# RMS norms of a two-layer decoder step: partial sums on VectorE, a root without ScalarE, and one tile per step for the second half's first norm

## Chip, cores and metric

The kernel runs on one core of a Trainium2 chip. The metric is device time in microseconds (us) of one execution.

## What is computed

One inference step of a two-layer decoder on 1024 prompt tokens and 8 sequences of 8 sampled tokens. Layer 0 mixes tokens by stick-breaking attention, layer 1 by an RWKV-7 recurrence; each is followed by a squared-ReLU MLP. Every sub-layer starts with an RMS norm whose result is scaled and shifted by vectors computed from a conditioning input, and ends with a gated residual add:

```python
def rmsnorm(x, g):
    y = x * lax.rsqrt(jnp.mean(x * x, axis=-1, keepdims=True) + 1e-6)
    return y * g
...
for i in range(2):
    hp, gp = ada_norm(xp, c, norm_mix[i], ...)      # norm 0 (attention), norm 2 (RWKV)
    xp = xp + gp * mixer(hp)                        # w_o is the mixer's last matmul
    hp, gp = ada_norm(xp, c, norm_ffn[i], ...)      # norms 1 and 3
    u = relu(hp @ w_up[i])
    xp = xp + gp * ((u * u) @ w_down[i])
y = rmsnorm(xp, final_norm)                         # the final norm
```

## The kernel before

**Tiling.** Activations lie transposed: 8 tiles of 128 features by tokens. The 1088 tokens are cut into half A (576, all prompt) and half B (448 prompt and 64 sampled tokens). Each half has 5 norms, so there are 10. They are called 0A, 0B, 1A, 2A, 1B, 2B, 3A, 3B, FA and FB below (F: final), which is their order in time except that FA comes just behind 3B.

**A dense layer** (`dense`, L346 to L362) is done in three products, because each fp32 operand is split into a high and a low part: for each output tile `m` and each stretch of tokens, 8 steps of three matmuls into `dq` (L358 high by high, L359 weight by low part of the input, L360 low part of the weight). The weights are split as they come: ScalarE casts `wh` (L342), GpSimd and VectorE subtract `wl` (L344, L345). After each step `self.step` lets other work go on by its rate: attention, then the RWKV units (`rw_units`, whose VectorE rows here are L1046 to L1163, and their triangular inverses `rw_lanes`, L1205 to L1214), then the RWKV chains. The evacuation of `w_o` and `w_down` is `residual` (L363): VectorE adds gate times `dq` to the x tile (L373); for sampled tokens VectorE makes `rs` (L376) and GpSimd adds it (L379).

**A norm** (`rms`, L258) squares the 8 tiles of x on ScalarE (`sq`, L265) and sums over features on TensorE: 4 matmuls with a matrix of ones for each tile, 32 in all, into `ssq` (L267). A program's fp32 matmul shows as two records. ScalarE takes a square root (L271), and VectorE turns it into a reciprocal root with one Newton step (L272 to L277, tile `rv`). Four matmuls spread the result over the partitions (`rb`, L281), and four copies, alternately on ScalarE and VectorE, make the tile `R`. Then `norm_tiles` makes for each tile x times R (`hf`, L291 on VectorE; for sampled tokens L295 to L297 on GpSimd), adds the shift and splits into `hhi` (ScalarE, L323 and L132) and `hlo` (VectorE L324, GpSimd L304); `rw_norm` does the like for norm 2 (`h`). The next dense layer's first matmul needs the first `hhi`, its second matmul the first `hlo`.

**Order.** The kernel is written with a tile framework whose scheduler sets the order of the instructions on each engine; each engine then works through its own list in that order. While half A goes through its first dense layers, the norm of half B's input runs beside it (`second`, at rate 1/5 of a step): all of `rms` in one step of that generator, then one tile of the norm per step. x is streamed for it tile by tile (`Passing`, L102, DMAs issued by SyncE). FA runs beside the last MLP of half B.

## Time and profile before

| | |
|---|---|
| median of 3 runs | 3694.59 us (3686.51 to 3700.34) |
| the profiled execution | 3691.91 us, of which its span is 3690.2 us |
| mean granted TensorE clock | 0.967 |
| busy share: TensorE, VectorE, ScalarE, GpSimd | 94%, 63%, 43%, 33% |
| instructions in all | 72202 |
| start of the ten square roots (L271) in norm order 0A to FB | 16.9, 67.7, 734.1, 1370.4, 1791.8, 2272.8, 2638.4, 3295.7, 3320.8, 3677.1 us |

The profile is one execution. Engines: PE is TensorE's matmul, PEld its weight load, DVE is VectorE, ACT is ScalarE, POOL is GpSimd, SP is SyncE. L267 is line 267 of the kernel. In a row of a timeline stand start, duration, engine, line, operation, output and inputs, and in square brackets how long the engine was idle before it and what ended that. A row of the waits names who waited for whom, the total, the number of times and the longest. PEclk is the clock granted to TensorE as a share of full speed. Idle time costs something only where TensorE, the busiest engine, has to wait.

### The profile page before, as it was taken

How to read it: one execution, taken by the hardware profiler on the slowest of the kernel's cores; microseconds unless marked ns; L12 is line 12 of the kernel's file. 1: busy time of each engine (PE TensorE's matmuls, PEld its weight loads, DVE VectorE, ACT ScalarE, POOL GpSimd, SP SyncE). 2: the span in 40 equal slices, each digit the busy share in tenths (PEclk: the TensorE clock that was granted, in tenths of full speed). 3: DMA queues.
4: the chain of work that ended last, by engine and by line, in shares of the span. 5: the costliest groups of instructions: out<-in, count | busy, mean ns of one | idle time of the engine just before them, and what ended most of it. 6: DMA issues, size and time to landing. Idle time of an engine off the chain costs nothing. (4 is left out here: it accounts for less than half of the span.)

```text
span 3690.2 us, 72202 instructions
## 1 busy us (share of the span) xinstructions
PE 3482.2 (94%) x26360; PEld 2770.2 (75%) x26360; DVE 2306.5 (63%) x4718; ACT 1602.1 (43%) x3342; POOL 1223.3 (33%) x1692
## 2 busy tenths in 40 slices
PE   7999999999999999988799998998899999989998
PEld 5986667778888876766577776666788888867887
DVE  4357678885554446687845557657884666645444
ACT  4255566663333345634334445543433444432332
POOL 2344434342222223223433335323222222343332
PEclk8999999999999999988899998999899999989999
DMA  6466653319977785667254445657345444433332
GB/s 237 147 218 209 208 182 121 96 38 333 350 290 263 276 315 174 206 192 210 79 155 133 122 153 159 192 190 219 117 132 144 140 132 122 125 113 114 95 95 83
DMA packets 433014, 634.54 MB, mean 172 GB/s; under 512 B 144337, under 2 KB 244562, under 8 KB 432658
## 3 DMA queue, kind: packets, MB, share of 16 engines
q1 hardware_dynamic: 369394, 532.90, 44.8%
q10 hardware_dynamic: 63264, 97.02, 7.9%
q8 instruction: 209, 3.42, 0.4%
q14 instruction: 147, 1.20, 0.1%
HBM read 523.76 MB, written 106.01 MB: 171 GB/s over the span
## 5 line engine op out<-in xcount | busy, mean ns | idle before, releaser
L344 POOL TENSOR_TENSOR wl<-wst,wh 128x256 fp32r<-128x256 f32 (+1 forms) x512 | 652.7, 1276 | 1432.1 <-ACT wh L342 1214.9
L342 ACT CAST wh<-wst 128x512 fp32r<-128x512 f32 (+1 forms) x512 | 424.5, 834 | 709.9 <-PE dq L359 570.2
L358 PE MATMUL dq<-hhi,wh 128*128 128x288 f32 (+1 forms) x2112 | 711.5, 337 | 21.1 <-ACT hhi L132 19.1
L359 PE MATMUL dq<-hlo,wh 128*128 128x288 f32 (+1 forms) x2112 | 704.0, 334 | 3.7 <-DVE hlo L324 2.9
L360 PE MATMUL dq<-hhi,wl 128*128 128x288 f32 (+1 forms) x2112 | 703.2, 333 | 0.0
L345 DVE TENSOR_TENSOR wl<-wst,wh 128x256 fp32r<-128x256 f32 (+1 forms) x512 | 358.8, 703 | 258.7 <-ACT wh L342 230.4
L358 PE MATMUL dq<-uh,wh 128*128 128x288 f32 (+1 forms) x1536 | 508.9, 336 | 5.3 <-ACT uh L472 2.2
L359 PE MATMUL dq<-ul,wh 128*128 128x288 f32 (+1 forms) x1536 | 507.2, 331 | 0.0
L360 PE MATMUL dq<-uh,wl 128*128 128x288 f32 (+1 forms) x1536 | 505.4, 332 | 0.0
L358 PEld LDWEIGHTS dq<-hhi,wh 128*128 128x128 f32 x2112 | 400.9, 190 | 71.0 <-ACT hhi L132 19.7
L359 PEld LDWEIGHTS dq<-hlo,wh 128*128 128x128 f32 x2112 | 401.0, 190 | 43.3 <-issue 9.3
L360 PEld LDWEIGHTS dq<-hhi,wl 128*128 128x128 f32 x2112 | 400.5, 190 | 36.2 <-issue 6.9
L373 DVE SCALAR_TENSOR_TENSOR x<-dq,mod,x 128x288 f32<-128x288 f32 (+1 forms) x432 | 245.2, 569 | 258.6 <-PE dq L360 255.5
L358 PEld LDWEIGHTS dq<-uh,wh 128*128 128x128 f32 x1536 | 288.1, 188 | 53.6 <-issue 18.0
L548 DVE TENSOR_TENSOR_SCAN prod<-prod 128x256 f32<-128x256 f32 (+5 forms) x264 | 247.9, 941 | 118.0 <-ACT prod L539 76.8
L360 PEld LDWEIGHTS dq<-uh,wl 128*128 128x128 f32 x1536 | 288.4, 188 | 29.6 <-issue 7.1
L359 PEld LDWEIGHTS dq<-ul,wh 128*128 128x128 f32 x1536 | 288.8, 188 | 27.6 <-issue 5.7
L358 PE MATMUL dq<-xhi,wh 128*128 128x288 f32 (+1 forms) x576 | 203.1, 353 | 4.8 <-ACT dn L132 1.8
L359 PE MATMUL dq<-xlo,wh 128*128 128x288 f32 (+1 forms) x576 | 199.7, 347 | 5.8 <-POOL xlo L304 3.9
L360 PE MATMUL dq<-xhi,wl 128*128 128x288 f32 (+1 forms) x576 | 197.5, 343 | 0.0
L470 DVE TENSOR_TENSOR ut<-ut 128x288 f32<-128x288 f32 (+1 forms) x192 | 154.2, 803 | 53.0 <-ACT ut L469 50.1
L472 ACT CAST uh<-ut 128x288 fp32r<-128x288 f32 (+1 forms) x192 | 94.8, 495 | 181.6 <-DVE ut L470 181.2
(300 smaller groups left out, 6234.7 us busy)
## 6 DMA issues: line engine op xcount, KB each, us to landing
pagek<-cache_kT SPq DMA_DIRECT2D x128, 512.0 KB
pagev<-cache_v SPq DMA_DIRECT2D x128, 512.0 KB
adaw<-ada_w SPq DMA_DIRECT2D x192, 256.0 KB
wst<-w_up SPq DMA_DIRECT2D x96, 512.0 KB
wst<-w_down SPq DMA_DIRECT2D x192, 256.0 KB
st<-s_st SPq DMA_DIRECT2D x40, 672.0 KB
wst<-sb_w_qkv SPq DMA_DIRECT2D x48, 512.0 KB
wst<-w_up ACTq DMA_DIRECT2D x32, 512.0 KB
```

The lines of the kernel that those rows point to most:

```text
L342: nc.scalar.copy(wh, st)
L344: nc.gpsimd.tensor_sub(wl[:, :h], st[:, :h], wh[:, :h].bitcast(F32))
L345: nc.vector.tensor_sub(wl[:, h:], st[:, h:], wh[:, h:].bitcast(F32))
L358: nc.tensor.matmul(q, wh[:, k, :], h, start=k == 0, stop=False)
L359: nc.tensor.matmul(q, wh[:, k, :], l, start=False, stop=False)
L360: nc.tensor.matmul(q, wl[:, k, :], h, start=False, stop=k == kt - 1)
L373: nc.vector.scalar_tensor_tensor(xs, q[:, :np_], g, xs, ALU.mult, ALU.add)
L470: nc.vector.tensor_mul(t[:, :n], t[:, :n], t[:, :n])
L472: nc.scalar.copy(a, t[:, :n])
L548: nc.vector.tensor_tensor_scan(r, r, r, 1.0 if carry is None else carry, ALU.mult, ALU.bypass)
```

## The change

- `rms` no longer squares all tiles itself. An object `Sums` takes each tile of x as it is finished: ScalarE squares it as before, VectorE adds the square to a running tile (tiles 1 to 6; tile 7 is kept apart), so that 8 matmuls are left of 32. `residual` calls it when a tile of x is complete (w_o, and the last of the eight blocks of w_down).
- The reciprocal root is made on VectorE alone: an integer shift and a subtraction from a constant as first guess, then three Newton steps of three instructions.
- `R` is copied in two pieces of half its width, one by ScalarE and one by VectorE.
- The add for sampled tokens moves from GpSimd to VectorE (new line 409).
- `second` gives up its turn after each tile of x, so that its squares spread over nine steps.
- FA's norm is computed behind the last MLP of half A, its 8 products and output DMAs run beside w_o of half B at rate 0.25, where they ran beside the last MLP of half B at rate 1.

```diff
+class Sums:
+    def add(self, xf):
+        sq = tile(tag="n") if self.n else tile(tag="R", bufs=2)
+        nc.scalar.activation(sq, xf, AF.Square)
+        if self.n == 0:
+            self.acc = sq
+        elif self.n < NT - 1:
+            nc.vector.tensor_add(self.acc, self.acc, sq)
+        else:
+            self.last = sq
+        self.n += 1
...
-    def rms(self, x, pt, tmp, ps, tag, slot, rslot=None):
+    def rms(self, x, pt, tmp, ps, tag, sums=None):
...
-        for f in range(NT):
-            sq = tmp.tile([128, W], F32, tag=slot, name="sq")
-            nc.scalar.activation(sq, x[f], AF.Square)
+        for j, sq in enumerate((sums.acc, sums.last)):
             for g in range(4):
                 nc.tensor.matmul(q[32 * g:32 * g + 32, :w], self.ones32, sq[:, w * g:w * g + w],
-                                 start=f == 0, stop=f == NT - 1)
-        nc.scalar.activation(r, q[:, :w], AF.Sqrt, bias=self.eps, scale=1.0 / D)
-        nc.vector.tensor_scalar(ms, q[:, :w], 1.0 / D, EPS, ALU.mult, ALU.add)
-        nc.vector.reciprocal(y, r)
-        nc.vector.tensor_mul(t, y, y)
-        nc.vector.tensor_mul(t, t, ms)
-        nc.vector.tensor_scalar(t, t, -0.5, 1.5, ALU.mult, ALU.add)
-        nc.vector.tensor_mul(r, y, t)
-        for g in range(4):
+                                 start=j == 0, stop=j == 1)
+        nc.vector.tensor_scalar(t, q[:, :w], 1.0 / D, EPS, ALU.mult, ALU.add)
+        self.rsqrt(r, t, y)
+        for h in range(2):
             qb = ps.tile([128, 512], F32, tag=tag, name="rb")
-            nc.tensor.matmul(qb[:, :w], ...)
-            self.copy(R[:, w * g:w * g + w], qb[:, :w])
+            for g in range(2):
+                nc.tensor.matmul(qb[:, w * g:w * g + w], ...)
+            self.copy(R[:, 2 * w * h:2 * w * h + 2 * w], qb[:, :2 * w], "av"[h])
...
+    def rsqrt(self, r, t, y):
+        nc.vector.tensor_scalar(y.bitcast(I32), t.bitcast(I32), 1, None, ALU.arith_shift_right)
+        nc.vector.tensor_scalar(r.bitcast(I32), y.bitcast(I32), -1.0, float(0x5f3759df), ALU.mult, ALU.add)
+        for _ in range(3):
+            nc.vector.tensor_mul(y, r, r)
+            nc.vector.scalar_tensor_tensor(y, y, -0.5, t, ALU.mult, ALU.mult)
+            nc.vector.scalar_tensor_tensor(r, y, 1.5, r, ALU.add, ALU.mult)
...
-                nc.gpsimd.tensor_add(xv, xv, t)
+                nc.vector.tensor_add(xv, xv, t)
+            if sums and c0 + n == pt.W:
+                sums.add(x[m])
...
-            self.RB = self.rms(Passing(self, I["x"], B, tmp), B, tmp, ps, "aux", "n", "R")
+            x, sums = Passing(self, I["x"], B, tmp), Sums(self, B, tmp)
+            for f in range(NT):
+                sums.add(x[f])
+                yield
+            self.RB = self.rms(None, B, tmp, ps, "aux", sums)
...
+            self.behind(self.final(x, rms(x, A, sumsA), A), 0.25)
             dense(I["rw_w_o"], y, B, self.residual(2, xB, B, tmp, sums))
-            R = rms(xB, B)
-            self.behind(self.final(x, A, tmp, PS))
-            self.ffn(3, xB, *norm(3, xB, R, B), B, hp, tmp, PS)
+            self.until(lambda: False)
+            R = rms(xB, B, sums)
+            self.ffn(3, xB, *norm(3, xB, R, B), B, hp, tmp, PS, sums)
```

How the order of the instructions moves is shown at three places; the line numbers in front are those of the kernel the rows come from, "x24" counts equal instructions in a row. First TensorE in norm 0B, inside the first dense layer (`dq`, lines 358 to 360 before, 388 to 390 now), before the change:

```order
L360 MATMUL dq<-hhi,wl 128x288
L267 MATMUL ssq<-sq,ones_62 32x128 x24
L281 MATMUL rb<-rv,cst 128x128 x4
L358 MATMUL dq<-hhi,wh 128x288
L359 MATMUL dq<-hlo,wh 128x288
```

And with the change, where the 57 `dq` rows between the two pieces are left out:

```order
L390 MATMUL dq<-hhi,wl 128x288
L289 MATMUL ssq<-sq,ones_62 32x128 x8
L388 MATMUL dq<-hhi,wh 128x288
...
L390 MATMUL dq<-hhi,wl 128x288
L300 MATMUL rb<-rv,cst 128x128 x4
L388 MATMUL dq<-hhi,wh 128x288
```

Before, the last 24 sums and the four `rb` followed each other with nothing between; now 57 matmuls of the dense layer stand between the sums and `rb`.

Second VectorE at norm 3A, where units and lanes of the RWKV layer run beside w_o (`tm`, `lxn`: lanes; `kv`, `kk`: units). The root before:

```order
L272 TENSOR_SCALAR rv<-ssq 128x144
L273 RECIPROCAL rv<-rv 128x144
L1054 SCALAR_TENSOR_TENSOR kv<-kv 128x128
L1212 TENSOR_TENSOR lxn<-lxn,tm 128x8x24
L274 TENSOR_TENSOR rv<-rv 128x144
L1210 TENSOR_TENSOR tm<-llt,lxn 128x175
L1061 SCALAR_TENSOR_TENSOR kk<-k,par,kb 128x128
L275 TENSOR_TENSOR rv<-rv 128x144
```

The first rows of the root now (before's L1210, L1212 and L1046 are lines 1242, 1244 and 1078):

```order
L308 TENSOR_SCALAR rv<-rv 128x144
L1242 TENSOR_TENSOR tm<-llt,lxn 128x247
L309 TENSOR_SCALAR rv<-rv 128x144
L1244 TENSOR_TENSOR lxn<-lxn,tm 128x19x13
L312 TENSOR_TENSOR rv<-rv 128x144
L1242 TENSOR_TENSOR tm<-llt,lxn 128x252
L313 SCALAR_TENSOR_TENSOR rv<-rv 128x144
L1244 TENSOR_TENSOR lxn<-lxn,tm 128x18x14
L1078 TENSOR_SCALAR kv<-kq 128x128
```

Each link of the root still stands among work of the units and lanes, but there are 12 links where there were 6: 33 rows of other work stand between the first link and the copy of R now, and 16 before.

Third TensorE where w_o of half B begins. Before, `dq<-uh` (the last of w_down A) was followed by `dq<-shi` (the first of w_o B), and FA stood among the rows of the last MLP:

```order
L358 MATMUL dq<-hhi,wh 128x512
L267 MATMUL ssq<-sq,ones_62 32x144 x24
L359 MATMUL dq<-hlo,wh 128x512
L360 MATMUL dq<-hhi,wl 128x512
L358 MATMUL dq<-hhi,wh 128x512
```

Now all of FA's matmuls stand between the two dense layers:

```order
L390 MATMUL dq<-uh,wl 128x288
L289 MATMUL ssq<-sq,ones_62 32x144 x8
L300 MATMUL rb<-rv,cst 128x144 x4
L388 MATMUL dq<-shi,wh 128x512
L389 MATMUL dq<-slo,wh 128x512
```

So FA's sums and `rb` now stand between two dense layers, and no longer inside one.

More of the change, by code (lines that the diff above doesn't have):

```diff
@@ L274, in rms @@
-        nc.vector.tensor_mul(t, y, y)
-        nc.vector.tensor_mul(t, t, ms)
-        nc.vector.tensor_scalar(t, t, -0.5, 1.5, ALU.mult, ALU.add)
-        nc.vector.tensor_mul(r, y, t)
-        R = tmp.tile([128, W], F32, tag=rslot or slot, name="R", bufs=2 if rslot else None)
-        for g in range(4):
-            qb = ps.tile([128, 512], F32, tag=tag, name="rb")
-            nc.tensor.matmul(qb[:, :w], self.cst[:, C_SELB + 128 * g:C_SELB + 128 * g + 128], r,
-                             start=True, stop=True)
-            self.copy(R[:, w * g:w * g + w], qb[:, :w])
@@ L284, in rms @@
-        return R
+                                 start=j == 0, stop=j == 1)
+        v = tmp.tile([128, 3, w], F32, tag="n", name="rv")
+        t, r, y = (v[:, i, :] for i in range(3))
+        nc.vector.tensor_scalar(t, q[:, :w], 1.0 / D, EPS, ALU.mult, ALU.add)
+        self.rsqrt(r, t, y)
+        R = tmp.tile([128, W], F32, tag="R", name="R", bufs=2)
+        for h in range(2):
+            qb = ps.tile([128, 512], F32, tag=tag, name="rb")
+            for g in range(2):
+                sel = C_SELB + 128 * (2 * h + g)
+                nc.tensor.matmul(qb[:, w * g:w * g + w], self.cst[:, sel:sel + 128], r, start=True,
+                                 stop=True)
+            self.copy(R[:, 2 * w * h:2 * w * h + 2 * w], qb[:, :2 * w], "av"[h])
@@ L362, in dense, with residual @@
                 evac(m, c0, n, q)
-    def residual(self, s, x, pt, tmp):
+    def residual(self, s, x, pt, tmp, sums=None):
         nc = self.nc
@@ L454, in ahead, with ffn @@
         yield
-    def ffn(self, s, x, hi, lo, pt, pool, tmp, ps):
+    def ffn(self, s, x, hi, lo, pt, pool, tmp, ps, sums):
         nc, I = self.nc, self.I
         wu, wd = I["w_up"][s // 2], I["w_down"][s // 2]
-        res = self.residual(s, x, pt, tmp)
+        res = [self.residual(s, x, pt, tmp, sums if b == 7 else None) for b in range(8)]
         for b in range(8):
@@ L1580, in second @@
         def second(ps):
-            self.RB = self.rms(Passing(self, I["x"], B, tmp), B, tmp, ps, "aux", "n", "R")
+            x, sums = Passing(self, I["x"], B, tmp), Sums(self, B, tmp)
+            for f in range(NT):
+                sums.add(x[f])
+                yield
+            self.RB = self.rms(None, B, tmp, ps, "aux", sums)
             yield
@@ L1612, in rest @@
         x, o = self.next
-        dense(I["sb_w_o"], o, A, self.residual(0, x, A, tmp))
+        sums = Sq(A)
+        dense(I["sb_w_o"], o, A, self.residual(0, x, A, tmp, sums))
         self.show("x1", x, A)
-        R = rms(x, A)
+        R = rms(x, A, sums)
         self.rw_setup(lp)
-        self.ffn(1, x, *norm(1, x, R, A), A, hp, tmp, PS)
+        sums = Sq(A)
+        self.ffn(1, x, *norm(1, x, R, A), A, hp, tmp, PS, sums)
         self.show("x2", x, A)
@@ L1622, in rest @@
         self.ready.add("rw")
-        R = rms(x, A)
+        R = rms(x, A, sums)
         r = self.rw_norm(x, R, A, hp, tmp)
@@ L1627, in rest @@
         x, o = self.next
-        dense(I["sb_w_o"], o, B, self.residual(0, x, B, tmp))
-        RB = rms(x, B)
-        self.ffn(1, x, *norm(1, x, RB, B), B, hp, tmp, PS)
+        sums = Sq(B)
+        dense(I["sb_w_o"], o, B, self.residual(0, x, B, tmp, sums))
+        RB = rms(x, B, sums)
+        sums = Sq(B)
+        self.ffn(1, x, *norm(1, x, RB, B), B, hp, tmp, PS, sums)
         self.show("x2", x, B)
         self.spill(x, B)
-        R = rms(x, B)
+        R = rms(x, B, sums)
         r = self.rw_norm(x, R, B, hp, tmp)
@@ L1639, in rest @@
         x, y = self.next
-        dense(I["rw_w_o"], y, A, self.residual(2, x, A, tmp))
+        sums = Sq(A)
+        dense(I["rw_w_o"], y, A, self.residual(2, x, A, tmp, sums))
         self.show("x3", x, A)
-        R = rms(x, A)
-        self.ffn(3, x, *norm(3, x, R, A), A, hp, tmp, PS)
+        R = rms(x, A, sums)
+        sumsA = Sq(A)
+        self.ffn(3, x, *norm(3, x, R, A), A, hp, tmp, PS, sumsA)
         self.until(lambda: False)
@@ L1650, in rest @@
                 pass
-            dense(I["rw_w_o"], y, B, self.residual(2, xB, B, tmp))
+            self.behind(self.final(x, rms(x, A, sumsA), A), 0.25)
+            sums = Sq(B)
+            dense(I["rw_w_o"], y, B, self.residual(2, xB, B, tmp, sums))
             self.show("x3", xB, B)
-            R = rms(xB, B)
-            self.behind(self.final(x, A, tmp, PS))
-            self.ffn(3, xB, *norm(3, xB, R, B), B, hp, tmp, PS)
             self.until(lambda: False)
-            for _ in self.final(xB, B, tmp, PS):
+            R = rms(xB, B, sums)
+            sums = Sq(B)
+            self.ffn(3, xB, *norm(3, xB, R, B), B, hp, tmp, PS, sums)
+            self.until(lambda: False)
+            for _ in self.final(xB, rms(xB, B, sums), B):
                 pass
```

20 lines of the change are left out of this document (13 added, 7 removed).

## The prediction

> **What bounds the kernel now.** I read the page first, then the granted clock, then one table of stretches around the ten norms, then the waits inside those stretches.
>
> ```profile
> PE 3482.2 (94%) x26360; PEld 2770.2 (75%) x26360; DVE 2306.5 (63%) x4718; ACT 1602.1 (43%) x3342; POOL 1223.3 (33%) x1692
> PEclk8999999999999999988899998999899999989999
> ```
>
> TensorE is busy 3482.2 of the 3690.2 us span; the other 208 us and the stretches at a lower clock are all that a change can win, apart from matmuls taken away. The next view sums stretches; columns are the stretch, its length, busy time and instructions of PE, PEld, DVE, ACT and POOL, then the granted clock, DMA share and rate.
>
> ```profile
> core 0: us, PE busy (x) PEld busy (x) DVE busy (x) ACT busy (x) POOL busy (x), PEclk, DMA share, GB/s
> 58.00:78.00 20.00, 10.01 (x76) 7.50 (x71) 7.59 (x15) 8.16 (x17) 6.58 (x11) 0.57 0.40 127
> 78.00:110.00 32.00, 32.00 (x244) 32.00 (x243) 16.36 (x22) 11.54 (x22) 19.26 (x29) 1.00 0.49 166
> 715.00:765.00 50.00, 43.42 (x351) 32.64 (x350) 45.83 (x66) 39.74 (x73) 19.94 (x36) 0.90 0.12 36
> 1365.00:1400.00 35.00, 24.16 (x243) 12.41 (x241) 25.19 (x40) 23.65 (x40) 13.20 (x16) 0.78 0.92 360
> 1768.00:1812.00 44.00, 23.53 (x168) 17.52 (x168) 29.66 (x67) 15.33 (x33) 18.77 (x30) 0.69 0.37 100
> 2250.00:2300.00 50.00, 42.16 (x441) 28.81 (x440) 40.04 (x106) 33.07 (x83) 33.13 (x68) 0.80 0.70 228
> 2630.00:2655.00 25.00, 13.71 (x139) 11.58 (x138) 24.69 (x62) 10.79 (x17) 4.80 (x8) 0.71 0.22 64
> 3240.00:3260.00 20.00, 20.00 (x119) 17.73 (x118) 5.67 (x11) 4.75 (x6) 7.09 (x5) 1.00 0.73 255
> 3290.00:3310.00 20.00, 6.65 (x80) 4.56 (x78) 11.64 (x22) 7.29 (x16) 10.86 (x21) 0.65 0.09 26
> 3310.00:3331.00 21.00, 16.24 (x106) 11.69 (x107) 12.17 (x21) 10.07 (x21) 7.62 (x15) 0.77 0.11 34
> ```
>
> By their places the rows are 0B, a stretch of undisturbed dense work, 1A, 2A, 1B, 2B, 3A, the start of half B's second w_o, 3B and FA. Undisturbed, TensorE is busy throughout at full clock; at the norms it is idle for up to two thirds of the time, and what it does there runs at 0.57 to 0.90 of the clock. So time is won and lost at the norms, and a microsecond of waiting costs somewhat more than one, by the clock that sinks with it. The share of an engine over the whole span says nothing here; it matters that VectorE is 92% busy around 1A, 80% around 2B and 99% around 3A (24.69 of 25), so that work added to it there comes out late, while at 0B, 1B and 3B it has room.
>
> **Part by part.** The prices first, from the tile of the root (count, then shortest, median and longest in ns, first and last start):
>
> ```profile
> L271 ACT ACTIVATE rv<-ssq,eps x10: 367/374/382, 16.9 to 3677.1; 128x144 f32<-128x144 f32 x5, 128x128 f32<-128x128 f32 x5
> L271 ACT ACT_TABLE_LOAD  x5: 1283/1283/1283, 15.6 to 2637.1; - x5
> L273 DVE RECIPROCAL rv<-rv x10: 942/994/1043, 17.6 to 3677.7; 128x144 f32<-128x144 f32 x5, 128x128 f32<-128x128 f32 x5
> L274 DVE TENSOR_TENSOR rv<-rv x10: 277/293/1368, 18.8 to 3678.7; 128x144 f32<-128x144 f32 x5, 128x128 f32<-128x128 f32 x5
> L276 DVE TENSOR_SCALAR rv<-rv x10: 203/227/235, 19.7 to 3679.3; 128x144 f32<-128x144 f32 x5, 128x128 f32<-128x128 f32 x5
> ```
>
> The root before: 0.37 on ScalarE, then two tensor-scalar steps, a reciprocal and three products on VectorE, 2 x 0.23 + 0.99 + 3 x 0.29 = 2.3. The root now: 3 x 0.23 + 9 x 0.29 = 3.3, if a scalar-tensor-tensor of 128x144 takes what a product does (the trace has none of that shape). So each root costs VectorE 1.0 us more and the chain 0.6 more, without a table load; at the five norms with a table load the chain gains 1.28 less 0.6, if ScalarE was what it waited for.
>
> The page "ScalarE: Activation LUTs" of the Trainium skill, under "What ACT_TABLE_LOAD costs", adds a drain of about 1.38 us to the load; by it 1B and 2A would each gain 1.4 more than below. I keep the row's 1.28.
>
> *0B.* Here TensorE waited for the squares, and then for the root:
>
> ```profile
> PE ssq L267 <- ACT sq L265: 6.3, 4, 3.3
> PE rb L281 <- DVE rv L277: 3.1, 1, 3.1
> ```
>
> In the 20 us from 58 TensorE was busy 10.01 at a clock of 0.57, which is 5.7 us of full-clock work, a part of it the old `ssq` and `rb`. So at least 14.3 us are lost. With the change the squares come one tile per step, and 57 matmuls stand between the sums and `rb`: at 32.00/244 = 0.13 us each they last 7.5 us, and the root with one `wl` between its links (0.7) needs 4. Nothing waits there any longer, provided the eight x tiles land in time; what is late next is the normalised tile, which is not needed before half A's dense layer ends. Of the stretch's rows, `ssq` falls to a quarter and `rb` stays, about 1 us. I take **-15**; the bounds are 0 (the tiles land late and the same wait appears) and -17 (all that is idle or slow).
>
> *1B.* Three waits in a row, and on VectorE the reason for one of them:
>
> ```profile
> PE dq L358 <- ACT hhi L132: 11.0, 1, 11.0
> PE s L1146 <- ACT L L1163: 4.9, 1, 4.9
> PE rb L281 <- DVE rv L277: 3.6, 1, 3.6
> ```
>
> ```profile
> 1775.77 0.75 DVE L1130 TENSOR_TENSOR BK<-k,Gi 128x576 f32<-128x576 f32 x1
> 1776.44 0.67 DVE L373 SCALAR_TENSOR_TENSOR x<-dq,mod,x 128x448 f32<-128x448 f32 x1
> 1777.03 0.21 DVE L376 TENSOR_TENSOR rs<-dq,mod 128x64 f32<-128x64 f32 x1
> 1777.16 0.68 DVE L345 TENSOR_TENSOR wl<-wst,wh 128x512 fp32r<-128x512 f32 x1
> 1780.70 0.91 DVE L1205 MEMSET lxn<- 72x1024 f32 x1 [2.87 <-DMA s_xn<-lxn]
> 1781.69 0.65 DVE L373 SCALAR_TENSOR_TENSOR x<-dq,mod,x 128x448 f32<-128x448 f32 x1
> 1792.19 0.29 DVE L272 TENSOR_SCALAR rv<-ssq 128x128 f32<-128x128 f32 x1 [5.24 <-ACT rv L271]
> 1797.15 0.19 DVE L1210 TENSOR_TENSOR tm<-llt,lxn 72x31 f32<-72x31 f32 x1 [2.57 <-DMA llt<-s_l]
> 1798.46 0.78 DVE L291 SCALAR_TENSOR_TENSOR hf<-x,mod,R 128x448 f32<-128x448 f32 x1
> ```
>
> The last residual (1781.69) stood behind a memset that waited 2.87 us for a DMA. In the new order the memset stands behind the last residual, so the residual comes 2.87 + 0.91 = 3.8 earlier, less two more adds of 0.68 and two small ones of 0.21 ahead of it: 2. From the residual to the root's first step 10.5 us passed, 5.24 of them waiting for the square, its sums, the table load and the root. The adds and the load are off that path now; of 5.24 I count 3. The copies of R stood behind the lanes' wait for `llt` (2.57); now two `hf` go ahead of it. That sum is -7.6, but the lanes' DMA still lands when it lands and holds the later `hf` and the first `hlo`: I take **-6**, bounds -2 and -10.
>
> *1A, 2B, 3A.* Here VectorE is the engine that is full, and gets more: per norm six adds (0.75 for 576 columns and 0.68 for 512, by L1130 and L345 above, products and differences of two tiles) and 1.0 for the root, thus 5.5 us ahead of the first `hf`; at 2B also 8 x 0.21 for the small adds. Against that stand fewer sums on TensorE and, at 1A and 2A, a second table load on ScalarE, by which attention's sigmoid (L539) comes back:
>
> ```profile
> 3317.32 1.68 PE L267 MATMUL ssq<-sq,ones 128*32 128x144 f32 x48
> ```
>
> ```profile
> L539 ACT ACT_TABLE_LOAD  x3: 1283/1283/1283, 168.5 to 1370.8; - x3
> ```
>
> 48 of 64 records go at each norm, 0.035 each, 1.7 us where TensorE has something else to do; at 1A ScalarE gets back 2 x 1.28 + 0.37 = 2.9.
>
> At 3A, with VectorE at 99%, all 5.5 come out, less what the new order puts off: **+5** (0 to +9; above 5.5 if TensorE's clock sinks for longer). At 1A (92%) about 5 less 2.9: **+2** (-3 to +5). At 2B (80%) 6.5 of VectorE's time, with gaps that take up most of it, less 1.7: **+1.5** (-3 to +5).
>
> *2A.* The table load and the root (1.65) go from the path, the links cost 1.0 more, and ScalarE is free 1.28 earlier for attention's next sigmoid: **-1.5** (-5 to +2). *0A* lies beside the loading of the first weights, which take longer: 0, or the 1.0 of the longer root.
>
> *3B.* Here the first matmul waits 8.0 us, for sampled columns that GpSimd normalises in an order that the change leaves as it is (six L295, then six L296, then L297):
>
> ```profile
> PE dq L358 <- ACT hhi L132: 8.0, 1, 8.0
> ```
>
> ```profile
> 3301.13 3.61 POOL L295 TENSOR_TENSOR hf<-x,R 128x64 f32<-128x64 f32 x6 [6.60 <-DVE R L134]
> 3304.71 3.47 POOL L296 TENSOR_TENSOR hf<-hf,mod 128x64 f32<-128x64 f32 x6
> 3308.14 1.56 POOL L297 TENSOR_TENSOR hf<-hf,mod 128x64 f32<-128x64 f32 x6
> 3294.57 0.63 ACT L265 ACTIVATE sq<-x 128x512 f32<-128x512 f32 x1 [1.62 <-POOL x L379]
> ```
>
> The last square waited 1.62 for GpSimd's small add, which now takes 0.2 on VectorE; the longer root eats that: 0.
>
> *FA.* Before, inside the MLP, `rb` waited for the root (the sums' row stands above):
>
> ```profile
> 3325.99 1.78 PE L281 MATMUL rb<-rv,cst 128*128 128x144 f32 x8 [4.34 <-DVE rv L277]
> ```
>
> The stretch from 3310 to 3331 had 4.76 us idle and ran at 0.77, of 16.24 busy at most 3.7 were lost to the clock, and 2.2 of sums go. Now FA stands between w_down A and w_o B, where TensorE was busy 20.00 of 20: the last residual and its square (0.65 + 0.63 by L373 and L265, 1.5 with the hand-overs), 16 records of sums (0.5), root and one split tile (4.2), then `rb`; 6 us idle and about 2 at half clock. Gain 11 less 8: **-3.5** (-8 to +3). *FB* ends the program with the longer root: **+0.6**.
>
> Elsewhere the 144 small adds (30 us), 60 adds (43 us) and roots (10 us) are 83 us more for VectorE, under dense stretches such as 78 to 110, where it is half idle: 0. ScalarE still makes all 80 squares.
>
> The page "SBUF — State Buffer" of the Trainium skill speaks against this under "SBUF: two separate sides": VectorE instructions with two SBUF inputs hold a port pair that GpSimd's reads then wait for. By it each of the 60 adds could stop a `wl` on GpSimd for 0.7 us, 42 in all, and the sum would be +25 if TensorE waited for every one; the stretches above show no wait of TensorE for `wl`, so I leave it at 0.
>
> **Sum**: -15 - 6 + 5 + 2 + 1.5 - 1.5 - 3.5 + 0.6 = -16.9. The profiled execution took 3691.9 us, so 3675.0; the median of the runs shown is 2.7 higher, so 3677.7. I forecast 3676, from a start of 3693 between the two. The bound of what can be told from no change, 0.5%, is 18.5 us: 3676.1.
>
> **Rivals.**
>
> *The waits cost double.* Idle time at 0B and 1B also lowers the clock (0.57, 0.69); if 0B gains its full 17, 1B 10 and FA 8, and 1A comes out even, the sum is -29.4: 3663.6, say 3664. For it speaks the clock column; against it that the lanes' DMA at 1B does not move.
>
> *0B gains nothing.* The x tiles share SyncE's queue with the weights, and the squares wait for the tiles; if the dense layer now waits for late weights behind them, -16.9 becomes -2: 3691. DMA is busy 0.40 in that stretch, which speaks against it.
>
> *Slower: VectorE becomes the bound.* Its 83 us more lie partly where attention, units and chains run on it. From the point where more than half comes out on TensorE it outweighs the gains (26 us in all): at 0.55 it is +46 - 26 = +20, 3713. For it: 99% at 3A, 12 links that each queue behind other work. Against it: over the span VectorE is at 63%, and the adds of the last w_down block lie in dense work like that from 78 to 110, where it is at 51%.
>
> **Chances.** Forecast with its bounds 0.66, about evenly on both sides of 3676.1; doubled waits 0.14; no gain at 0B 0.10; VectorE-bound 0.10. Faster by over 0.5%: 0.32 + 0.14 = 0.46; within: 0.34 + 0.10 = 0.44; slower: 0.10. The range leaves out the last rival and the far ends: 3656 to 3700.
>
> **What would show it.** Right: no wait of `ssq` or `rb` between 45 and 80 us and a clock of 1.00 there; 1B's stretch from last residual to first `dq` shorter by about 6; 3A's longer by about 5; a gap of some 6 us before w_o B and none at 3326. Wrong: waits for squares or weights near 60 us, VectorE's waits growing in the attention and unit stretches, or 1A and 3A longer by 10 each.

## The result, and the profile after

| | before | after |
|---|---|---|
| median of 12 runs each | 3697.04 us (3686.51 to 3704.09) | 3711.02 us (3704.51 to 3716.62) |
| the profiled execution, and its span | 3691.91, 3690.2 us | 3713.59, 3711.8 us |
| mean granted TensorE clock | 0.967 | 0.959 |

The ratio after to before is 1.0038 with a 95% interval of 1.0027 to 1.0048: 14 us slower. That is still within the 0.5% that the prediction calls no change, but 35 us from its 3676 and above its range.

The page of after, busy times:

```profile
PE 3475.3 (94%) x25880; PEld 2775.5 (75%) x25880; DVE 2443.9 (66%) x4972; ACT 1588.5 (43%) x3314; POOL 1154.0 (31%) x1548
```

VectorE has 137 us more, GpSimd 69 less, TensorE 7 less. The next view shows the stretches that answer to those of the prediction, in the same columns. The rows are 0B, the 24 us behind it, 1A, 2A, 1B, 2B, 3A, FA in its new place, and 3B:

```profile
55.00:75.00 20.00, 19.96 (x161) 19.33 (x161) 11.80 (x14) 11.02 (x17) 7.68 (x6) 1.00 0.52 171
98.00:122.00 24.00, 18.80 (x132) 18.34 (x131) 13.27 (x19) 7.49 (x14) 13.75 (x20) 0.95 0.34 113
702.00:752.00 50.00, 39.17 (x307) 29.68 (x306) 46.56 (x70) 35.65 (x70) 20.35 (x38) 0.92 0.14 42
1352.00:1387.00 35.00, 23.99 (x211) 13.38 (x210) 29.05 (x46) 20.05 (x35) 12.98 (x17) 0.74 1.01 401
1757.00:1801.00 44.00, 26.33 (x142) 20.54 (x142) 36.58 (x91) 14.93 (x32) 18.79 (x27) 0.67 0.41 112
2232.00:2282.00 50.00, 38.77 (x385) 28.49 (x385) 44.67 (x110) 30.58 (x78) 28.99 (x59) 0.68 0.71 220
2605.00:2655.00 50.00, 32.51 (x236) 27.62 (x234) 49.20 (x122) 17.00 (x30) 7.70 (x11) 0.70 0.30 92
3255.00:3276.00 21.00, 3.15 (x28) 2.33 (x27) 12.85 (x21) 6.78 (x11) 6.69 (x5) 0.62 0.70 250
3322.00:3342.00 20.00, 4.68 (x28) 2.96 (x27) 13.98 (x28) 6.47 (x15) 10.96 (x21) 0.57 0.04 14
```

The 0B stretch is now full (19.96 of 20 at clock 1.00), and just behind it, where before was full, 5 us are idle. Before w_o of half B (3255) TensorE works 3.15 of 21 us.

The waits of TensorE for the norms, over the whole span. Before:

```profile
PE rb L281 <- DVE rv L277: 21.9, 8, 4.3
PE ssq L267 <- ACT sq L265: 19.7, 7, 8.7
```

After:

```profile
PE rb L300 <- DVE rv L314: 37.4, 6, 16.3
PE ssq L289 <- ACT sq L117: 5.2, 3, 3.2
```

The change did what it says for the sums: 14.5 us of waiting for ScalarE's squares are gone. Of these, 8.7 stood at the very start of the program; there TensorE now waits 13.9 us for a DMA (`adaw`), and the first dense matmul comes hardly earlier. The wait for the root took the place of the others, with 15.5 us more, and 16.3 of its total stand at a single spot.

Both kernels have 13824 matmuls into `dq`, in the same order of layers, so stages can be cut at the n-th of them. The table gives the length of each stage in us, read from the traces; `before_again` is a second profile of the kernel before, and the last four columns are experiments told below. Matmuls of units and chains can move from one stage to another, so a stage can also grow by work moved into it.

| stage (norm in it), `dq` no. | before | before_again | after | fa_slots | s_even | r_3A | n_ms |
|---|---|---|---|---|---|---|---|
| start to 1st | 38.4 | 44.1 | 37.7 | 38.9 | 43.7 | 43.4 | 37.3 |
| to 600 (0B) | 100.3 | 98.8 | 92.0 | 90.4 | 86.6 | 98.9 | 100.4 |
| to 2100 | 578.7 | 578.5 | 579.3 | 581.1 | 578.1 | 578.9 | 577.6 |
| to 5100 (1A) | 631.2 | 631.5 | 629.8 | 629.7 | 632.1 | 629.7 | 632.7 |
| to 6300 (2A, units) | 358.2 | 358.6 | 362.8 | 361.6 | 360.6 | 360.3 | 376.2 |
| to 6600 (1B) | 119.3 | 118.8 | 115.0 | 116.5 | 118.7 | 118.3 | 113.7 |
| to 8400 (2B) | 604.3 | 604.1 | 601.1 | 601.2 | 603.1 | 602.9 | 638.8 |
| to 9600 (units, 3A) | 321.8 | 329.3 | 336.5 | 340.1 | 326.4 | 332.2 | 319.8 |
| to 12000 (chains) | 478.6 | 478.2 | 484.3 | 481.1 | 481.8 | 492.4 | 479.0 |
| to 12400 (FA or its place, 3B) | 118.0 | 118.1 | 130.0 | 120.6 | 118.0 | 113.3 | 113.4 |
| to the end (FB) | 341.5 | 341.6 | 343.4 | 343.6 | 342.3 | 342.4 | 342.5 |

Two executions of before differ by 11.4 us: 5.7 until the first `dq` and 7.5 in the stage with 3A, in both at a lower clock (0.81 and 0.96, 0.91 and 0.93). The rest agrees within 1.5. So the profile shown before the change is one of the quicker executions, and a stage is read here against both.

After gains 7 to 8 us at 0B and 4 at 1B. It loses 4 to 5 in the stage of 2A, 6 with the chains and 12 at 3B and FA. The two stages of 2B and 3A have to be taken together, since 48 chain matmuls (`qc`) moved from the first to the second: 937.6 us, against 926.1 and 933.4, so 4 to 12 more.

### The profile page after: what moved, and what is told of

It reads as the page before. It is cut to its first block, busy times and chain, and to the rows that moved or that the text cites. A ratio compares the mean times of both kernels' runs of the same rounds, so it can differ in the third digit from the quotient of the medians.

```text
span 3711.8 us, 71372 instructions
## 1 busy us (share of the span) xinstructions
PE 3475.3 (94%) x25880; PEld 2775.5 (75%) x25880; DVE 2443.9 (66%) x4972; ACT 1588.5 (43%) x3314; POOL 1154.0 (31%) x1548
## 4 chain that ended last, share of the span: by engine, by line
PE 40%; DVE 7%; DMA 2%; issue 2%; SPq 1%; POOL 1%; ACT 1%; ACTq 0%; DVEq 0%; POOLq 0%
PE dq L388 11%; PE dq L389 11%; PE dq L390 11%; DVE lxn L1244 1%; PE qc L1361 1%; DVE tm L1242 1%; PE qc L1351 1%; PE qc L1370 1%; SPq L1249 1%; DVE wl L375 1%; PE yq L1518 0%; PE qc L1365 0%; PE qc L1374 0%; PE bonq L1510 0%; DMA hv<-s_v 0%
## 5 line engine op out<-in xcount | busy, mean ns | idle before, releaser
L374 POOL TENSOR_TENSOR wl<-wst,wh 128x256 fp32r<-128x256 f32 (+1 forms) x512 | 638.3, 1249 | 1549.6 <-ACT wh L372 1331.4
```

The source lines that it names most:

```text
L374: nc.gpsimd.tensor_sub(wl[:, :h], st[:, :h], wh[:, :h].bitcast(F32))
```

## Experiments

All ratios are to the kernel before on the same chip, with 95% intervals. "Placed elsewhere" counts rows of TensorE's list of some 20800 that are not in the common order of the two kernels.

| run | against | placed elsewhere | median us | ratio to before |
|---|---|---|---|---|
| after | before | thousands | 3711.02 | 1.0038 [1.0027, 1.0048] |
| fa_slots | after | 33 | 3704.26 | 1.0010 [0.9997, 1.0022] |
| fa_back | after | 49 | 3702.76 | 1.0010 [0.9997, 1.0023] |
| old_root | after | 2339 | 3705.82 | 1.0009 [0.9995, 1.0022] |
| root_fa_back | after | 2353 | 3703.32 | 1.0005 [0.9993, 1.0018] |
| gps_add | after | 1889 | 3717.3 | 1.0057 [1.0040, 1.0075] |
| a_rev | after | 1298 | 3715.91 | 1.0034 [1.0019, 1.0049] |
| a_o3A | after | 653, from 3A on | 3707.92 | 1.0020 [1.0006, 1.0033] |
| b_second | before | 1169 | 3700.06 | 0.9999 [0.9987, 1.0012] |
| b_root | before | 2725 | 3734.79 | 1.0104 [1.0088, 1.0120] |
| b_adds | before | 2411 | 3719.57 | 1.0060 [1.0046, 1.0074] |
| n_rev | before | 1642 | 3697.84 | 0.9998 [0.9987, 1.0008] |
| n_late | before | 1098 | 3702.24 | 1.0004 [0.9995, 1.0013] |
| n_ms | before | 2416 | 3734.64 | 1.0098 [1.0083, 1.0113] |
| s_even | before | 12, at 0B | 3685.89 | 0.9971 [0.9957, 0.9984] |
| r_3A | before | 987, from 3A on | 3714.45 | 1.0042 [1.0027, 1.0057] |
| b_s3A | before | 853, from just ahead of 3A on | 3709.24 | 1.0022 [1.0009, 1.0035] |
| e_best | before | 16, at 0B and 2A | 3693.6 | 0.9979 [0.9964, 0.9995] |

### Why TensorE stands still before w_o of half B

After, TensorE's waits from 3255 to 3276, and VectorE there:

```profile
PE rb L300 <- DVE rv L314: 16.3, 1, 16.3
```

```profile
3264.12 0.69 DVE L334 TENSOR_TENSOR slo<-t,shi 128x512 fp32r<-128x512 f32 x1 [5.50 <-ACT shi L152]
3266.05 1.28 DVE L334 TENSOR_TENSOR slo<-t,shi 128x512 fp32r<-128x512 f32 x1 [1.24 <-ACT shi L152]
3267.43 0.31 DVE L293 TENSOR_SCALAR rv<-ssq 128x144 f32<-128x144 f32 x1
3267.78 0.77 DVE L308 TENSOR_SCALAR rv<-rv 128x144 int32<-128x144 int32 x1
3268.58 1.19 DVE L309 TENSOR_SCALAR rv<-rv 128x144 int32<-128x144 int32 x1
...
3271.99 1.42 DVE L314 SCALAR_TENSOR_TENSOR rv<-rv 128x144 f32<-128x144 f32 x1
...
3274.13 0.31 DVE L314 SCALAR_TENSOR_TENSOR rv<-rv 128x144 f32<-128x144 f32 x1
```

The root stands on VectorE behind two `slo`, the splits of half B's y tiles, and these waited for ScalarE's `shi`, which waited for the loads:

```profile
3263.47 0.62 ACT L152 CAST shi<-t 128x512 fp32r<-128x512 f32 x1 [5.76 <-DMA t<-s_y]
```

The loads of y as SyncE issues them, first before, then after:

```profile
3211.77 1.40 SPq L435 DMA_DIRECT2D t<-s_y  x3
3213.82 0.38 SPq L435 DMA_DIRECT2D t<-s_y  x1
...
3215.58 0.42 SPq L435 DMA_DIRECT2D t<-s_y  x1
...
3216.58 0.38 SPq L435 DMA_DIRECT2D t<-s_y  x1
```

```profile
3257.61 4.25 SPq L467 DMA_DIRECT2D t<-s_y  x6
3264.84 2.29 SPq L467 DMA_DIRECT2D t<-s_y  x2
```

Before, the loads of six of the eight y tiles were issued by 3217, 30 us ahead of w_o's first matmul (3247.8). After, all of them are issued once w_down is done. They land in tiles of the tag `n`, of which there are six; the squares of the last w_down block now use the same six (`Sums.add`, `tag="n"`). Two runs test this with the order otherwise kept.

**fa_slots**, the squares in the pool of split tiles:

```diff
...
-        sumsA = Sq(A)
+        sumsA = Sums(self, A, tmp, lambda: hp.tile([128, A.W], F32, tag="h", name="sq"))
```

> The changed kernel, but the squares of half A's last w_down block lie in the pool of split tiles and no longer in the six slots that the loads of half B's y tiles use. The wait before w_o of half B (16.3 us in the changed kernel) is put down to those loads. Theory (slots): with the squares out of the way six y tiles are loaded again beside w_down, from about 3210 to 3225 us, the wait of rb for the root falls from 16.3 to 6 or 7 us, and the ratio to the kernel before falls from 1.0038 to about 1.001 (3701 us). Rival (queue): the root is late because its twelve links stand on VectorE behind the splits, wherever the loads are; then the wait stays above 13 us and the time at 3709 us or more.

**fa_back**, the norm back in the last MLP:

```diff
-            self.behind(self.final(x, rms(x, A, sumsA), A), 0.25)
...
+            self.behind(self.final(x, lambda: rms(x, A), A))
             self.ffn(3, xB, *norm(3, xB, R, B), B, hp, tmp, PS, sums)
...
```

> The changed kernel with the final norm of half A back inside half B's last MLP at rate 1, all in one piece as before (its squares and adds made there); everything else as changed. Theory (the move costs): moved, it cost about 22 us before w_o of half B and gave 11 back inside the MLP, so this kernel is 11 us faster than the changed one: about 3700 us, ratio 1.001, with w_o of half B starting without a gap and a wait for the root of 4 to 5 us inside the MLP. Rival (the move is neutral, the loss only follows from half B's chains ending later): 3708 to 3712 us.

Both came out at 1.0010, 0.0028 or 10 us below after, as both theories had it. In fa_slots the loads are early again, and the wait is 9.3 us, not the 6 or 7 of the theory; SyncE's queue and TensorE's waits there:

```profile
3221.42 0.64 SPq L467 DMA_DIRECT2D t<-s_y  x1
3223.05 0.93 SPq L467 DMA_DIRECT2D t<-s_y  x2
```

```profile
PE rb L300 <- DVE rv L314: 9.3, 1, 9.3
```

So the tile slots cost 7 of the 16.3 us of that wait. The rest of the gap stays: from w_down's last matmul to w_o's first it is 13 us in fa_slots, 21 in after and none before, and the splits `shi`, which began at 3215 before, begin only at 3259 in fa_slots. The move itself, freed of the slots, is worth nothing that can be told: fa_slots and fa_back are equal.

### Parts undone or done alone

The next six take out or put in parts. Each also gave the scheduler, which orders by a simulated timeline, another program, and one to three thousand rows went elsewhere.

old_root (after, with before's lines 269 to 277 in place of 291 to 294, so the old root at all norms):

> The changed kernel with the square root on ScalarE and one Newton step on VectorE as before; sums, moves and copies as changed. Theory (links): at norm 3A the twelve links each queue behind units and lanes; with six links the 12.5 us from the first link to rb shrink to about 7, the start of MLP 3A comes 5 to 10 us earlier, and the five table loads and square roots give back 1 to 3: ratio 0.997 to 1.000 against the changed kernel, some 3701 to 3706 us. Rival (the sums, not the root): norm 3A stays as late as changed, and with the table loads the kernel is 3711 us or slower.

It came out at 1.0009, as the links theory had it; but in its profile the stage to the 8400th `dq` is 19 us longer than in after, and the ones of 3A and of FA are 18 and 11 shorter. So the order moved time about, and the root's share can't be read from it.

b_second (before, with `second` and its `Sums` as changed):

> The kernel before with one part of the change alone: the first norm of half B squares one tile per step and adds the squares on VectorE; roots, sums elsewhere, the final norm and GpSimd's adds as before. Theory (the part is worth what the changed kernel shows at 140 us, 9 us, because K pages and x tiles still land when they land): 3688 us, ratio 0.9975. The prediction's own size: 15 us, 3682 us, ratio 0.996. Rival (the gain there is lost again later, as any earlier start is at a wait for a DMA or for attention): 3695 us or more, ratio above 0.999.

0.9999, as the rival had it: 15 to 16 us are gained in the stage to the 600th `dq` in its profile, and nothing is left at the end. Outside 0B its instructions are those of before.

root_fa_back (old_root and fa_back together):

> The changed kernel with two parts undone together: the square root back on ScalarE with one Newton step, and the final norm of half A back inside half B's last MLP. Left of the change are half B's first norm one tile per step, the sums on VectorE, the copies of R in two pieces and the small adds on VectorE. Theory (the two losses are separate: links at norm 3A, tile slots before w_o of half B): they add, 1.0038 less 0.0029 less 0.0028 gives 0.998, about 3692 us. Rival (each undoing only moved the same late chains about): no better than either alone, 1.001, about 3703 us.

1.0005: the theory that the two losses add falls.

b_root (before, with the new root at all ten norms) and b_adds (before, with `Sums` in `residual` for seven norms):

> The kernel before with the new root alone (twelve links on VectorE, no square root on ScalarE, 32 sums on TensorE as before). Theory (links): at norm 3A the way from the first link to rb grows from 6.5 to 11 to 13 us, and the stage from there to the first MLP's middle is some 10 us longer; the table loads give 2 to 4 back: ratio 1.001 to 1.003, 3703 to 3710 us. The prediction's price (a root 1.0 us longer on VectorE, 0.6 on the chain, less 1.28 at five norms): 0.9985 to 1.000. Rival (the links hurt only together with the adds): within 0.0005 of 1.

> The kernel before with the adds alone: each finished tile of x is squared and VectorE adds the squares, 8 matmuls of sums instead of 32; roots, half B's first norm, the final norm of half A, GpSimd's small adds and the copies of R as before. Theory (the adds are not what loses): the squares leave the path at 1B and 2B, and the ratio is 0.997 to 1.000, 3688 to 3699 us. Rival (VectorE becomes the bound, as the prediction had it): 48 adds, 34 us, come out where units and chains run, ratio above 1.003.

b_root came out at 1.0104, off every expectation. Ten roots add 10 us to VectorE, and the time rose by 38. The theory of links does not give that, and a price per link fitted to it would have mixed in the order, as the controls show. b_adds came out at 1.0060: the theory that the adds do not lose falls, and the rival, VectorE as the bound, had forecast a ratio above 1.003. With 2411 rows elsewhere the run can't tell that rival from an effect of the order.

gps_add (after, `nc.gpsimd.tensor_add(xv, xv, t)` again):

> The changed kernel with the small adds for sampled tokens back on GpSimd; 1889 rows of TensorE stand elsewhere, from half B's first MLP on. Theory (144 adds of 0.2 us are no cost of their own): 1.0025 to 1.005, the difference from 1.0038 being the order's. Rival (30 us more on VectorE come out where units and chains run): 1.000 or below.

1.0057, a little above the theory's range: giving the small adds back to GpSimd did not help, against the rival. With 1889 rows elsewhere this is no price of the adds themselves.

### Controls: the same work in another order

before_again (no edit), one execution:

> The kernel before, unchanged, profiled once more, to see how far two executions of one kernel differ by stage. Theory (the profile shown of it is one of its faster executions, 3692 where the median is 3698): the same order of instructions, dense stages equal within 1 us, and 5 to 10 us more in the stages at a sinking clock: the second half of attention with the first mixer, and the RWKV units. Rival (executions differ evenly everywhere): each stage longer by about 0.2%.

It took 3703.27 us; its stages stand in the table beside those of before. The theory holds but for the place: start and 3A, not attention.

n_rev, n_late and n_ms write independent steps of the norm in another order; a_rev does so in after:

```diff
# n_rev
-        for g in range(4):
+        for g in (3, 2, 1, 0):
# n_ms
-        nc.scalar.activation(r, q[:, :w], AF.Sqrt, bias=self.eps, scale=1.0 / D)
         nc.vector.tensor_scalar(ms, q[:, :w], 1.0 / D, EPS, ALU.mult, ALU.add)
+        nc.scalar.activation(r, q[:, :w], AF.Sqrt, bias=self.eps, scale=1.0 / D)
# a_rev
-        for h in range(2):
+        for h in (1, 0):
```

> A control: the kernel before with the four rb matmuls and copies of every norm written in the reverse order of pieces. It has the same instructions on every engine, but the scheduler, which orders by a simulated timeline, places 1642 of 20826 rows of TensorE elsewhere. Theory (reshuffling): the order alone moves the time by as much as the whole change did, so the ratio to before lies 0.003 or more from 1, to either side. Rival (the order hardly matters, and each part of the change has its own price): within 0.0015 of 1.

> A second control: the kernel before with one step of the root, the mean square on VectorE, written two instructions later. Same instructions on every engine; 1098 rows of TensorE stand elsewhere. Theory (reshuffling): the ratio lies 0.003 or more from 1 in at least one of the three controls, with the loss in the attention-to-units and units-to-chains stages. Rival: within 0.0015 of 1.

> A third control: the kernel before with the mean square on VectorE written ahead of the square root on ScalarE instead of behind it. Same instructions but for 4 fewer table loads on ScalarE (5 us); 2416 rows of TensorE stand elsewhere, nearly as many as the new root moves (2725). Theory (reshuffling): the new root alone cost 38 us, though its links' own work is 10 us; if most of that is the order, this control is some 10 to 40 us slower as well, ratio 1.003 to 1.01. Rival (the links cost it): within 0.0015 of 1, or faster by the table loads.

> A control on the other side: the changed kernel with the two pieces of R in every norm written in the reverse order. Same instructions on every engine; 1298 rows of TensorE stand elsewhere. Theory (reshuffling): its time differs from the changed kernel's 1.0038 by 0.003 or more, to either side; the wait before w_o of half B stays (tile slots), the 25 us at norm 3A may go. Rival (the change's own parts cost it): 1.003 to 1.005, with the same loss at 3A.

n_rev, n_late and a_rev did nothing to the time that can be told; for n_rev and a_rev that is against the theory. n_ms, as its theory had it, cost 1%, as much as the new root alone (b_root). Its page has the counts of before, with 4 instructions less on ScalarE:

```profile
PE 3508.8 (94%) x26360; PEld 2793.3 (75%) x26360; DVE 2313.1 (62%) x4718; ACT 1600.0 (43%) x3338; POOL 1220.4 (33%) x1692
```

So the order is no steady noise: three of the four orders cost nothing that can be told, and one costs 36 us. n_ms and b_root share it. In both, 32 matmuls into `kq` (units) stand between the 6000th and 6300th `dq` where before has 24, and 592 and 576 into `qc` (chains) between the 6600th and 7200th where before has 328. Both lose 34 to 37 us up to the 8400th (the row of 2B). b_adds shares the first of the two marks, and its stretch from 6000 to 6300 is 12 us longer (125.1 to 113.0). That b_root's loss is the order's is likely by its likeness to n_ms, and not shown. The loss is no single wait: in the stage to the 8400th `dq`, TensorE of n_ms is idle 21.6 us where before has 15.5, has 106 rows more in the trace, and runs at a clock of 0.955 where it was 0.977. What in the order brings this about is not traced.

### With the order held

By choosing the edit so that the list of TensorE stays the same up to it, a part can be looked at by itself. In s_even and e_best the list behind it stays too, and the time is the part's. In r_3A, b_s3A and a_o3A the list behind it moves, so that their times hold the part and an order together.

**s_even**: 0B alone, on before, giving up its turn after every second tile.

```diff
             for f in range(NT):
                 sums.add(x[f])
-                yield
+                if f % 2:
+                    yield
```

> The kernel before with half B's first norm alone changed: its squares are added on VectorE and it gives up its turn after every second tile instead of after every tile. By this choice of step the scheduler leaves every row of TensorE behind the first 140 us where it was. Theory (the gain is real, and b_second lost it by its order): 8 to 14 us stay to the end, ratio 0.9965 to 0.998. Rival (an earlier start is lost at later waits, whatever the order): ratio above 0.999.

0.9971, 11 us faster than before, as the theory had it, and the lowest ratio of all runs. Its stretch and its waits from 45 to 140 us:

```profile
58.00:78.00 20.00, 17.90 (x143) 16.90 (x142) 13.46 (x18) 9.83 (x15) 8.22 (x5) 1.00 0.54 174
```

```profile
PE ssq L295 <- DVE sq L121: 1.5, 1, 1.5
PE dq L386 <- ACT dn L152: 0.7, 1, 0.7
PE rb L309 <- DVE rv L305: 0.6, 1, 0.6
```

The same part in b_second, with another order behind it, was worth nothing.

**r_3A** and **b_s3A**: before with the new root, or the adds, at norm 3A alone. **a_o3A**: after with the old root there alone.

> The kernel before with the new root at norm 3A alone; the order is before's up to that norm (2600 us). Theory (the links cost it): twelve links among lanes and units take 12 us from the first to rb where six took 6.5, and the stretch from the last w_o matmuls to the first 300 of the MLP is 6 to 12 us longer: ratio 1.001 to 1.003. Rival (the links alone do little, since only the adds before them fill VectorE): the stretch is longer by 2 us or less, ratio within 0.001 of 1.

> The kernel before with the adds at norm 3A alone (old root); order as before up to 2590 us. Theory (the adds cost less than the links): the last residual and the root start 2 to 4 us later, TensorE has 24 matmuls less; the stretch is 0 to 5 us longer, ratio within 0.0015 of 1. Rival (the adds cost it): 8 us or more, ratio above 1.002.

> The changed kernel with the old root at norm 3A alone; order as in the changed kernel up to that norm. Theory (the links cost it): the wait of rb for the root, 8.9 us, falls to 3 to 5, the stretch at 3A is 8 to 15 us shorter, and the ratio to the kernel before falls from 1.0038 to 1.000 to 1.002. Rival (the loss at 3A is the order around it, units placed there that were elsewhere before): 1.003 or more.

With the root alone it is 1.0042 (15.6 us), above the theory's range; with the adds alone 1.0022 (8 us), which is the rival's number; taken out of after, the root gives 0.0018 back, at the edge of the theory's range, and the interval overlaps with that of after. In a_o3A the wait of `rb` falls from 8.9 to 1.0 us, but the next matmul then waits 5.7 for `hhi`. TensorE at the norm, first before, then r_3A:

```profile
2637.18 0.71 PE L267 MATMUL ssq<-sq,ones 128*32 128x144 f32 x8 [2.86 <-ACT sq L265]
...
2645.33 2.29 PE L281 MATMUL rb<-rv,cst 128*128 128x144 f32 x8 [4.10 <-DVE rv L277]
2647.54 3.55 PE L1146 MATMUL s<-AR,BK 64*128 64x128 f32 x30
2651.02 0.65 PE L358 MATMUL dq<-hhi,wh 128*128 128x288 f32 x3
```

```profile
2641.21 0.71 PE L270 MATMUL ssq<-sq,ones 128*32 128x144 f32 x8 [2.85 <-ACT sq L268]
...
2650.20 3.75 PE L1167 MATMUL s<-AR,BK 64*128 64x128 f32 x30 [5.76 <-DVE BK L1151]
2653.88 1.41 PE L291 MATMUL rb<-rv,cst 128*128 128x144 f32 x6
...
2658.24 0.85 PE L291 MATMUL rb<-rv,cst 128*128 128x144 f32 x2
...
2666.08 1.09 PE L379 MATMUL dq<-hhi,wh 128*128 128x288 f32 x3 [1.22 <-ACT hhi L344]
```

Before, `rb` came ahead of the unit's `s`. Now 30 `s`, with a wait for `BK` of 5.76 us, stand ahead of `rb`, and the fourth `rb` stands behind more of the unit. The first and last link of the root on VectorE, in r_3A and then before:

```profile
2642.38 0.29 DVE L277 TENSOR_SCALAR rv<-ssq 128x144 f32<-128x144 f32 x1
...
2651.80 0.30 DVE L305 SCALAR_TENSOR_TENSOR rv<-rv 128x144 f32<-128x144 f32 x1
```

```profile
2638.86 0.31 DVE L272 TENSOR_SCALAR rv<-ssq 128x144 f32<-128x144 f32 x1
...
2644.97 0.30 DVE L277 TENSOR_TENSOR rv<-rv 128x144 f32<-128x144 f32 x1
```

The root takes 9.7 us where it took 6.4: 3.3 more, not 0.6 or 1.0. From the last sums to the first `dq` it is 24 us (2641.92 to 2666.08) and before 13 (2637.89 to 2651.02). So the links are 3 of the 11 us. `rb` comes later behind the unit's `s`, and its fourth piece behind more of the unit on TensorE's own list: 4 to 5 more. The last copy of `R` is the rest, 4. It stands on ScalarE behind copies of the unit that wait 3.87 us for a DMA, and VectorE waits for it:

```profile
2661.73 0.43 ACT L1199 COPY S<-bkq 128x320 f32<-128x320 f32 x1 [3.87 <-DMA s_st<-S]
...
2662.79 0.32 ACT L135 COPY R<-rb 128x144 f32<-128x144 f32 x1
2663.14 4.46 DVE L312 SCALAR_TENSOR_TENSOR hf<-x,mod,R 128x576 f32<-128x576 f32 x6 [3.71 <-ACT R L135]
```

By the stage table 14 us more lie with the chains behind, whose order moved too, and 4.7 come back at 3B. These two can come of the order alone: n_rev and n_late, whose times do not differ from before, have 490 us in the stage of the chains and 112 in that of 3B, against 478.6 and 118.0. b_s3A has 489.8 and 112.6, so its 8 us may be the order's for the most part, and a price of the adds at 3A is not shown.

**e_best**: s_even with the new root at 2A and 3B and the adds at 3B, all of which leave the order as it is.

> s_even (the kernel before with half B's first norm in steps of two tiles) with those parts of the change added that leave the order of TensorE as it is: the new root at norms 2A and 3B, and the adds at 3B. Theory (with the order held, a part costs or gains its own work and no more): a table load less at 2A, 24 sums less at 3B, 1 to 3 us together, so ratio 0.996 to 0.997, about 3685 us. Rival (links and adds cost by themselves, as at 3A): 0.999 or more, 3695 us.

0.9979 [0.9964, 0.9995]: not to be told from s_even. The number lies between the theory and the rival, and the interval reaches from one to the other. Where the order stays and no unit stands beside the norm, root and adds cost or bring too little to be told, a few us at most.

## Why the prediction was wrong

Three steps failed. The largest is FA's -3.5, which came out at +12 with 3B: the gap before w_o was taken as 6 us idle, and the wait there is 16.3, in part since the loads of half B's y tiles had lost their slots; fa_slots shows 7 us of the wait, and 10 us of time, to come of that. The second is the -15 of 0B, of which 7 to 8 are there in after's stage, since TensorE next waits for copies of `dq` that stand behind DMA waits on VectorE. The third is "Elsewhere ... 0": 6 us are lost with the chains and 4 to 5 with the units behind 2A. Behind it stands a habit of all terms: each edit was priced in the order of before, the new order was read for three places, and its effect on the rest was set to nothing. The runs show that the same work in another order can cost 1% (n_ms), and that a gain of 11 us (s_even) is there or not by a `yield` more or less (b_second). That the 6 and the 4 to 5 us come of the order is argued from this and not shown. By its terms:

- *0B, -15.* The cause was right: the waits for squares and root are gone, and by the 200th `dq` after is 18 us ahead. By the 600th it is 9. The term overlooked who is late next on VectorE. There the copies of `dq` (`dn`) now stand behind `hf` and `kk`, which wait for DMAs; VectorE's waits in after from 98 to 122 us, and TensorE's:

```profile
DVE hf L321 <- DMA x<-x: 6.2, 2, 3.2
DVE kk L556 <- DMA k<-kT: 5.0, 1, 5.0
```

```profile
PE dq L388 <- DVE dn L154: 5.2, 2, 3.6
```

  With the order held, the part is worth 11 (s_even).
- *1B, -6.* After is 4 us shorter in that stage: in its bounds. No run holds the order for it.
- *3A, +5 (0 to +9).* 4 to 12 in after with 2B, against the 6.5 of both terms; so the size held, and the mechanism only in part. The links were counted at their busy time on a full VectorE. What they cost is their places: other work stands between each two of them, and in r_3A a unit also went ahead of `rb` on TensorE and of the last copy of `R` on ScalarE. In after no unit holds `rb` up; there the root takes 12.5 us from its first link to `rb`, and TensorE's wait is

```profile
PE rb L300 <- DVE rv L314: 8.9, 1, 8.9
```

- *1A, +2 and 2A, -1.5.* -1.5 and +4 to 5 by stage, 2A with the units behind it. In e_best the new root at 2A brings no gain that can be told. The prediction's 1.28 us for a table load fits the rows: in before, 15 of the 20 loads start within 0.05 us behind ScalarE's instruction ahead of them, and each takes 1.283.
- *2B, +1.5.* Not to be told from 3A, since chain matmuls moved between the two stages; the size stays open.
- *FA, -3.5.* +12 with 3B. The 6 us of idle were 16.3, of which 7 go away when the squares leave the slots of the y tiles. The prediction looked at what stands on the engines' lists between w_down and w_o and not at who holds the buffers of the next loads. With that mended (fa_slots) the move is worth 0.
- *FB, +0.6:* +1.9. *3B, 0:* not told apart from FA; in e_best the stage is 0.8 longer.

The slower rival gave 3713, and the time is 3711, but its mechanism is not shown, and in part refuted. It made VectorE's extra time the price, 83 us, and that is even 137. (By its own numbers, 26 us of gain are outweighed when about a third of the 83 comes out, not half.) The greatest loss, FA's, is one of tile slots and not of VectorE's time, gps_add takes 144 adds away without a gain, and e_best adds some without a loss. b_adds came out as this rival would have it, with an order of its own. What is right in it is the place, 3A, where VectorE is full. The rival that 0B gains nothing is refuted by s_even as to the norm, though b_second shows how it can look like it. The waits did not cost double.

The Trainium skill's page "SBUF — State Buffer" (section "SBUF: two separate sides") was weighed in the prediction as 42 us on GpSimd. Its rule is an exclusive lock on a pair of ports: of a GpSimd instruction and a VectorE instruction that has two inputs in SBUF or runs in a two-port mode, the one that starts first holds the pair to its end, and the other waits. Here it is seen from the other end. In the rows before w_o above, `L308`, `L309` and one `L314` took 0.77, 1.19 and 1.42 us, while their kinds take 0.23, 0.23 and 0.29 in the median. GpSimd's rows at the time:

```profile
3265.52 4.16 POOL L334 TENSOR_TENSOR slo<-t,shi 128x512 fp32r<-128x512 f32 x3 [7.44 <-ACT shi L152]
3271.98 1.26 POOL L334 TENSOR_TENSOR slo<-t,shi 128x512 fp32r<-128x512 f32 x1 [2.31 <-ACT shi L152]
```

The three long ones end at 3268.55, 3269.77 and 3273.41, each within 0.2 us behind the end of one of GpSimd's (3268.45, 3269.68 and 3273.24). So the trace agrees with the lock, and here it is VectorE that paid, 2.6 us of FA's wait. `L314` has two inputs; `L308` and `L309` have one, and no run shows in which mode they ran. That it is this lock is argued from the times; no run took GpSimd away from this spot.

Two parts are shown by runs that nearly hold the order: 0B -11 and the slots +10. Less sure are the root at 3A, +7 to +16, and the adds there, +8, both with the order behind them in the number, and 1B, -4, by its stage alone. That makes +10 to +19, and +14 was measured; with terms of such width the agreement is partly luck, and root_fa_back shows that parts do not add.

## What to carry to other kernels

Where a scheduler orders the program by a simulated timeline, an edit is two changes, its work and a new order everywhere. Before pricing the work, compare the lists for the whole program, and time a control that moves the order without work; then look for a form of the edit that leaves the list alone, as `yield` after every second tile did. A chain of short instructions on a shared engine costs its places in the queue and what the scheduler lets pass ahead of its end, not its busy time. A tile taken from a rotating pool also takes a slot from the next load in that pool, so look at when loads are issued, not only at when they are needed.

## What was not expected of the hardware

Two executions of the same kernel (before) differ by 11 us in two places: 5.7 us until the first matmul of the first dense layer, and 7.5 us in the stage with 3A. In both places the slower execution is idle about as long as the other (15.7 and 14.6 us, 35.6 and 37.6) and its granted clock is lower (0.81 and 0.96, 0.91 and 0.93). The medians of before over the sets of runs are 3697 to 3700 us, and its single runs reach from 3687 to 3718.

The small adds on VectorE, priced at 0.21 us and 30 us in all, took 81. In after's groups by line (count, then busy us in all and mean ns of one):

```profile
L409 DVE TENSOR_TENSOR x<-x,rs 128x64 f32<-128x64 f32 x144 | 80.7, 560 | 0.6
```

The median of one is 0.22 us, the longest 1.32. By the trace 52 of the 144 took over 0.4 us. Each of these 52 started while an instruction of GpSimd was running and ended 0.08 to 0.09 us behind the end of that instruction; of the 92 short ones 12 started beside one. With the 60 adds of squares (50.5 us, where 43 were priced) this makes up most of VectorE's 137 us.
